# Spreading the DRAM sums of weight tiles over a two-layer decoder trunk, with one seven-product group moved from layer 0 to layer 1

## The chip, the cores and the metric

The kernel runs on one core of a Trainium2 chip. The metric is the device time of one execution in microseconds (us). Three runs of the kernel before took 819.1, 819.68 and 822.92 us; the median is 819.68.

## The reference

A residual stream x of 256 tokens by 1024 features goes through two layers, all in float32:

```python
for l in range(2):
    h = rms_norm(x, norm_mix[l])
    x = x + (short_conv_mixer(h) if l == 0 else moba_attention(h, shared K/V))
    x = x + mem_cross_attention(rms_norm(x, norm_mem[l]), rms_norm(mem, norm_memkv[l]))
    h = rms_norm(x, norm_ffn[l])
    g, u = split(h @ ffn_w_gu[l])          # 1024 x 5632: gate and up, 2816 each
    x = x + (silu(g) * u) @ ffn_w_down[l]  # 2816 x 1024
    if l == 0: shared K/V = rms_norm(x, kv_norm) @ w_kv, rotary on K
out = rms_norm(x, norm_final)
```

The change touches only the product h @ ffn_w_gu, the gate/up product of the two feed-forwards, and the transfers that prepare it.

## The kernel before

**Precision.** Every float32 operand is split into a high and a low part in fp32r; a product is three matmuls (low with high, high with low, high with high). A weight tile is loaded by SyncE as `raw` (512 KB), ScalarE casts it to `hi`, VectorE computes `lo` = raw - hi, and TensorE uses both. All matmuls have line 322, all work of ScalarE and VectorE has line 106 (helpers that record each operation), the weight loads line 339.

**Order of the work.** The program is written out by a planner at build time. `plan` is a list of 284 weight tiles ("items") in the order in which TensorE takes them, and `feed` loads, splits and hands them out. Up to five raw tiles and ten split pairs exist at a time (`RAWS`, `WBUFS`), so loads run ahead of TensorE by up to some ten to fifteen items. A clock model in the planner decides where in the streams of ScalarE and VectorE the splits stand; every engine then runs its stream strictly in order. `feed.hooks[n]` holds functions that are called right before the load of item n is issued; in this way other transfers are queued between loads. The items are: 0 to 63 the memory keys, convolution, memory values, query and output weights of layer 0; then the feed-forward of layer 0 (from 64 on); then 64 items for K, Q, V, memory keys (`memk1`), O, memory values, memory queries and output of layer 1; then the feed-forward of layer 1.

**The feed-forward.** The 2816 columns of gate and of up are cut into 11 pairs `jp` of 2 x 128 columns. Pairs 0 and 1 are computed by token rows (tiles `wr`), the others by columns (`wg` and `wu`, four items a pair). Between them stand the products with `ffn_w_down` (tiles `wd`, TensorE output `ff`), two pairs late; the last three pairs' down products follow at the end.

**Groups.** `GROUPS` names pairs that are computed two at a time, jp and jp + 1, with seven products instead of eight. The weights of a group make a 2 x 2 block matrix: `B11`, `B12` are gate and up columns for the upper 512 features, `B21`, `B22` those for the lower 512. A Strassen-like scheme (`seven`) takes three of the quarters as they are and four sums of them, T1 to T4, with sums S1 to S4 of the token activations on the other side. A group takes 14 weight tiles where two pairs take 8; the four down tiles of its two down products stand between them. Before, `GROUPS = (4, 8)` holds for both layers.

**The sums T1 to T4** don't depend on the input. They are built in DRAM by DMA, long before their group, in 16 steps of 512 KB for a group (`sum_steps`, 64 in all):

```python
order = (("T1", "B11", False), ("T3", "B12", False), ("T1", "B12", True), ("T3", "B22", True),
         ("T2", "T1", False), ("T2", "B22", True), ("T4", "T2", False), ("T4", "B21", True))
return [step(name, source, i, add) for name, source, add in order for i in range(2)]
```

A step with False is a plain DRAM-to-DRAM copy, issued by SyncE (line 453) in the same queue as the weight loads; one with True adds a quarter to a sum in DRAM, issued by GpSimd (line 452) with `accum_op`. An add waits for the copy that it adds to, and a copy of one sum from another waits for the adds of the first; the issuing engine stands while it waits. In the trace all sums are called `T`, and the tiles loaded from them `raw_wT`. GpSimd also computes the reciprocal roots of the norms (`rs`, line 106) and loads the stored activations of the memory for layer 1 (`mT`, line 1538, two halves).

Before, the steps hang at items 44 to 169: the first four copies of a group at four items in a row, then three items after each add, 32 items for a group.

Of the kernel before, what the change touches and what calls it, by code (L numbers as in the profile page):

```python
# [32 lines left out]
ROW_PAIRS = 2  # L33
# [6 lines left out]
HOLD = 300  # L40
AMPLE = 2
BANKWISE = 5
GROUPS = (4, 8)
SUMS_FROM = 44
SUM_GAP = 3


class Clock:
# [213 lines left out]
def yoco_kernel(  # L262
# [87 lines left out]
    def col_plan(name, w, c0):  # L350
        return [dict(name=f"{name}_{g}", src=w[g * 512:(g + 1) * 512, c0:c0 + T], a=4, b=T, gain=None, pieces=1,
                     halves=2) for g in range(2)]

    def pair_plan(name, w, c0):

        return [dict(name=f"{name}_{g}", a=2, b=2 * T, gain=None, pieces=1, halves=1,
                     src=[w[g * 256:(g + 1) * 256, c:c + T] for c in (c0, DFF + c0)]) for g in range(4)]
# [43 lines left out]
    def ffn_steps():  # L401

        steps = []
        for jp in range(NP):
            steps.append(("gu", jp))
            if ROW_PAIRS <= jp < NP - LAG + ROW_PAIRS:
                steps.append(("down", jp - ROW_PAIRS))
        return steps, list(range(NP - LAG, NP))
# [7 lines left out]
    def quarter(l, jp, name, i):  # L416
        kh, part = QUARTER[name]
        k = 4 * kh + 2 * i
        src = ffn_w_gu[l][k * P:(k + 2) * P, part * DFF + jp * T:part * DFF + jp * T + 2 * T]
        return src.rearrange("(a p) n -> p a n", p=P)  # L420

    def seven_plan(l, jp):
        plan = []
        for name in SEVEN:
            if name[:4] == "down":
                plan += down_plan(l, jp - ROW_PAIRS + int(name[4]))
                continue
            for i in range(2):
                it = dict(name=f"w{name}_{l}_{jp}_{i}", a=2, b=2 * T, gain=None, pieces=1, halves=1)
                if name[0] == "T":  # L430
                    it["sum"] = l, jp, name, i
                else:
                    kh, part = QUARTER[name]
                    k, c = 4 * kh + 2 * i, part * DFF + jp * T
                    it["src"] = ffn_w_gu[l][k * P:(k + 2) * P, c:c + 2 * T]
                plan.append(it)
        return plan
# [5 lines left out]
    def sum_steps(l, jp):  # L443
        for name in ("T1", "T2", "T3", "T4"):
            for i in range(2):
                weight_sums[l, jp, name, i] = aside.tile([P, 2, 2 * T], F32, name=f"{name}_{l}_{jp}_{i}")

        def step(name, source, i, add):
            dst = weight_sums[l, jp, name, i]
            src = weight_sums[l, jp, source, i] if source[0] == "T" else quarter(l, jp, source, i)  # L450
            if add:
                return lambda: nc.gpsimd.dma_start(dst, src, accum_op=OP.add)  # L452
            return lambda: nc.sync.dma_start(dst, src)
# [5 lines that stand above are left out]
    def down_plan(l, jp):  # L459
        return [dict(name=f"wd{l}_{k}", src=ffn_w_down[l][k * P:(k + 1) * P, :], a=1, b=D, gain=None, pieces=1,  # L460
                     halves=2) for k in (2 * jp, 2 * jp + 1)]

    def ffn_plan(l):
        steps, last = ffn_steps()
        plan = []
        for kind, jp in steps + [("down", jp) for jp in last]:
            if kind == "gu" and jp in GROUPS:
                plan += seven_plan(l, jp)
            elif kind == "gu" and jp - 1 in GROUPS or kind == "down" and \
                    any(jp + ROW_PAIRS - g in (0, 1) for g in GROUPS):  # L470
                pass
            elif kind == "gu" and jp < ROW_PAIRS:
                plan += pair_plan(f"wr{l}_{jp}", ffn_w_gu[l], jp * T)
            elif kind == "gu":
                plan += col_plan(f"wg{l}_{jp}", ffn_w_gu[l], jp * T)
                plan += col_plan(f"wu{l}_{jp}", ffn_w_gu[l], DFF + jp * T)
            else:
                plan += down_plan(l, jp)
        return plan
# [8 lines left out]
    plan += row_plan("cout", conv_w_out[0], 0) + row_plan("memv0", mem_w_kv[0], D, "memkv0")  # L488
    plan += q_plan(0) + row_plan("mo0", mem_w_o[0], 0)
    plan += ffn_plan(0)  # L490
    plan += row_plan("k1", w_kv, 0, "kv") + row_plan("q1", moba_w_q[0], 0, "mix1") + row_plan("v1", w_kv, D, "kv")
    plan += row_plan("memk1", mem_w_kv[1], 0, "memkv1", halves=2) + row_plan("o1", moba_w_o[0], 0)
    plan += row_plan("memv1", mem_w_kv[1], D, "memkv1")
    plan += q_plan(1) + row_plan("mo1", mem_w_o[1], 0)
    plan += ffn_plan(1)
    feed = side.feed = Feed(clock, plan, load_chunk, split_high, split_low)

# [452 lines left out]
    for k in range(KD):  # L950
        feed.hooks[36 + k] = [put_aside(k)]

    at = SUMS_FROM
    for l in range(2):
        for jp in GROUPS:
            for n, step in enumerate(sum_steps(l, jp)):
                feed.hooks.setdefault(at, []).append(step)
                at += SUM_GAP if n // 2 in (2, 3, 5, 7) else 1


    def short_conv(act, into):
# [175 lines left out]
    def swiglu(l, src, done, fine_end=False, at_end=None):  # L1137
# [8 lines left out]
        def gu_w(jp):  # L1146
            taken = {}

            def part(i):
                if i not in taken:  # L1150
                    taken[i] = [feed.take(f"{('wg', 'wu')[i]}{l}_{jp}_{g}") for g in range(2)]
                return taken[i]

            return part
# [41 lines left out]
        def gate_up(jp, w, jj):  # L1196
            u, j = unit_of(2 * jp + jj)
            pieces = [feat.tile([P, T], F32, tag=f"f{i}", name=f"gu_sb{i}") for i in range(2)]
            gus = []
            for i in range(2):  # L1200
                side.grab("gu")
                gus.append(gu_tile("gu"))
                mm_cols(gus[i], act, w(i), jj, 0)
            for i in range(2):
                mm_cols(gus[i], act, w(i), jj, 1)
                if jj:
                    feed.free(2)
                if i == 0:
                    gate = side.start(gate_steps(gus[0], pieces[0]))
                else:  # L1210
                    job = side.start(up_steps(gus[1], pieces, gate, u[:, j, 0, :], u[:, j, 1, :]))
            for h in range(2):
                guT.add_job(h, (2 * jp + jj) // 4, job)
# [170 lines left out]
        def down_w(jp):  # L1384
            return [feed.take(f"wd{l}_{2 * jp + i}") for i in range(2)]

        def down(jp, w, h, b, acc=None, c=(0, 512), first=0, end=NP - 1):
            for i in range(2):
                k = 2 * jp + i
                guT.need(k, (h,))  # L1390
                mm3(accs[h][b][:, c[0]:c[1]] if acc is None else acc, guT.parts(k, tok(h)),
                    [r[:, 0, b * 512 + c[0]:b * 512 + c[1]] for r in w[i]],
                    k == 2 * first, k == 2 * end + 1)
                side.poll()
# [6 lines left out]
        steps, last = ffn_steps()  # L1401
        sums_job = [side.start(token_sums())]
        for jp in range(ROW_PAIRS, NP):
            if jp in GROUPS:
                seven(jp)
            if jp in GROUPS or jp - 1 in GROUPS:
                continue
            w = gu_w(jp)
            n = jp - ROW_PAIRS
            gate_up(jp, w, 0)  # L1410
            wd = down_w(n) if ("down", n) in steps else None
            for h in range(2):
                if h == 1:
                    gate_up(jp, w, 1)
                for b in range(2 if wd else 0):
                    if h == b == 1:
                        feed.free(2)
                    down(n, wd, h, b)
# [186 lines left out]
    memv0 = mem_values("memv0", mT0)  # L1605
    mem_attention(0, memk0, memv0, in_mem0, in_ffn0)
    swiglu(0, in_ffn0, residual(in_moba))
    memk1, mT1 = moba(in_moba, in_mem1)
    memv1 = mem_values("memv1", mT1)
    mem_attention(1, memk1, memv1, in_mem1, in_ffn1)  # L1610
    swiglu(1, in_ffn1, finish, fine_end=True, at_end=lambda: fin.update(gain=load_gain(norm_final, "g_final")))


# [20 lines left out]
```

## Time and profile before

| | |
|---|---|
| median of three runs | 819.68 us |
| the profiled execution | 820.24 us |
| span of its trace | 818.5 us |
| TensorE busy, mean granted clock | 788.8 us (96%), 0.983 |
| VectorE, ScalarE, GpSimd busy | 580.4, 463.2, 51.8 us |
| DMA | 192.67 MB, 235 GB/s over the span |
| sums in DRAM | 16 + 16 copies by SyncE, 32 adds by GpSimd, 512 KB each |

In the rows of the trace PE is TensorE, DVE VectorE, ACT ScalarE, POOL GpSimd and SP SyncE; a q behind the name is the engine's sequencer, which issues DMAs. `out<-in` names what is written and what is read, without buffer numbers, and xN is the number of instructions. A row of the chain or of the timeline begins with its start and its length in us. In the timeline the brackets hold the time in which the engine stood before, and what ended it; "issue" there means that the profile shows nothing that it waited for. In a row of the stages stand the bounds, the length, then for PE, PEld (weight loads of TensorE), DVE, ACT and POOL the busy time and the number of instructions, then TensorE's granted clock (1.00 is full), the share of the 16 DMA engines that was busy, and GB/s.

### The profile page before, as it was taken

The page shows a single profiled execution, that of the slowest core. Times are in us where ns is not written, and L with a number is a line of the kernel's source. Part 1 is how long each engine was busy: PE and PEld are TensorE (multiplying, and loading weights), DVE is VectorE, ACT ScalarE, POOL GpSimd, SP SyncE. Part 2 cuts the span into 40 slices and gives each one's busy share as a digit, 9 for nine tenths or more (in the row PEclk, how much of TensorE's full clock was granted, in tenths as well). Part 3 has the DMA queues.
Part 4 walks back from the last instruction along what each step waited for, and adds up shares of the span by engine and source line. Part 5 has one row for each costly group of instructions (what it writes and reads, how often), then busy time and mean ns, then how long its engine had stood idle before and what let it go on. Part 6 is the DMA issues. An engine that isn't in the chain of part 4 may idle for free.

```text
span 818.5 us, 11285 instructions
## 1 busy us (share of the span) xinstructions
PE 788.8 (96%) x4141; PEld 672.5 (82%) x4141; DVE 580.4 (71%) x864; ACT 463.2 (57%) x721; POOL 51.8 (6%) x76
## 2 busy tenths in 40 slices
PE   9999999999989988996999999999999999999996
PEld 8988887898778867875788889988988788888885
DVE  5988786676676773676667566877767686966873
ACT  6765655665554643554556555655556555755751
POOL 0100011101110011011121100000000000000000
PEclk9999999999999988998999999999999999999999
DMA  9767799986988999899998942856543546965941
GB/s 333 224 213 230 245 319 226 370 216 155 284 227 277 306 321 297 215 358 289 342 281 252 253 172 97 263 204 203 205 134 104 185 151 216 323 206 189 330 150 51
DMA packets 99724, 192.67 MB, mean 235 GB/s; under 512 B 6669, under 2 KB 56917, under 8 KB 99157
## 3 DMA queue, kind: packets, MB, share of 16 engines
q1 hardware_dynamic: 90212, 172.54, 61.4%
q0 software_dynamic: 8992, 18.88, 12.9%
q8 instruction: 32, 0.52, 0.3%
q10 hardware_dynamic: 464, 0.53, 0.2%
q14 instruction: 24, 0.19, 0.1%
HBM read 188.78 MB, written 36.70 MB: 275 GB/s over the span
## 4 chain that ended last, share of the span: by engine, by line
PE 78%; DMA 12%; DVE 5%; ACT 2%; issue 2%; POOL 0%; SPq 0%; POOLq 0%; DVEq 0%; ACTq 0%
PE gu L322 15%; PE ff L322 11%; PE acc_memk L322 6%; PE q_acc L322 5%; PE cu L322 5%; PE acc_mo L322 5%; PE seven L322 5%; DMA raw_wd<-in_ffn_w_down_dram 4%; PE acc_memv L322 4%; PE pb L322 3%; PE acc_k L322 3%; PE acc_o L322 3%; DMA raw_wu<-in_ffn_w_gu_dram 3%; PE po L322 2%; DMA raw_wg<-in_ffn_w_gu_dram 2%; PE acc_v L322 2%
## 5 line engine op out<-in xcount | busy, mean ns | idle before, releaser
L322 PE MATMUL ff<-hi_wd,guT 128*128 128x512 f32 (+1 forms) x352 | 109.0, 391 | 0.0
L322 PEld LDWEIGHTS ff<-hi_wd,guT 128*128 128x128 f32 x352 | 66.9, 191 | 13.4
L322 PE MATMUL ff<-lo_wd,guT 128*128 128x512 f32 (+1 forms) x176 | 69.4, 394 | 0.0
L106 ACT CAST hi_wd<-raw_wd 128x1024 fp32r<-128x1024 f32 x44 | 46.1, 1050 | 19.4 <-DMA raw_wd<-in_ffn_w_down_dram 17.9
L106 DVE TENSOR_TENSOR lo_wd<-raw_wd,hi_wd 128x1024 fp32r<-128x1024 f32 x44 | 53.4, 1218 | 5.0 <-ACT hi_wd L106 4.5
L452 POOL DMA_DIRECT2D T<-in_ffn_w_gu_dram x32 | 33.9, 1059 | 268.8 <-issue 137.0
L106 DVE TENSOR_TENSOR gu_sb<-gu_sb,gu 128x256 f32<-128x256 f32 x40 | 16.6, 419 | 46.7 <-ACT gu_sb L106 46.5
L322 PE MATMUL gu<-ffn,hi_wg 128*128 128x512 f32 x160 | 44.2, 415 | 4.6 <-DVE gu_sb L106 4.6
L322 PE MATMUL acc_memk<-mT,hi_memk 128*128 128x256 f32 x256 | 47.0, 289 | 0.0
L106 ACT COPY gu_sb<-gu 128x256 f32<-128x256 f32 x40 | 14.7, 372 | 53.6 <-PE gu L322 53.4
L106 DVE TENSOR_TENSOR lo_wT<-raw_wT,hi_wT 128x1024 fp32r<-128x1024 f32 x32 | 38.2, 1220 | 8.2 <-ACT hi_wT L106 8.2
L322 PE MATMUL gu<-ffn,hi_wu 128*128 128x512 f32 x160 | 41.9, 406 | 0.0
L106 POOL TENSOR_TENSOR rs<-ms,neg_half 128x1 f32<-128x1 f32 x14 | 13.3, 948 | 448.6 <-DVE ms L106 447.1
L322 PE MATMUL acc_mo<-hi_mo,oT_mem 128*128 128x512 f32 x128 | 41.2, 397 | 0.2 <-DVE oT_mem L106 0.2
L322 PEld LDWEIGHTS gu<-ffn,hi_wg 128*128 128x128 f32 x160 | 31.2, 199 | 11.6 <-DVE gu_sb L106 5.4
L106 ACT CAST hi_wT<-raw_wT 128x1024 fp32r<-128x1024 f32 x32 | 33.1, 1052 | 12.6 <-DMA raw_wT<-T 12.4
L322 PEld LDWEIGHTS acc_memk<-mT,hi_memk 128*128 128x128 f32 x256 | 40.0, 196 | 0.2
L322 PE MATMUL gu<-hi_wr,ffn 128*128 128x512 f32 x128 | 39.8, 392 | 0.0
L322 PE MATMUL acc_memv<-hi_memv,mT 128*128 128x512 f32 x128 | 39.7, 391 | 0.0
L106 DVE TENSOR_TENSOR lo_wu<-raw_wu,hi_wu 128x1024 fp32r<-128x1024 f32 x28 | 33.7, 1220 | 8.0 <-ACT hi_wu L106 8.0
L322 PEld LDWEIGHTS ff<-lo_wd,guT 128*128 128x128 f32 x176 | 33.7, 191 | 6.6
L106 ACT CAST hi_wu<-raw_wu 128x1024 fp32r<-128x1024 f32 x28 | 29.3, 1051 | 15.4 <-DMA raw_wu<-in_ffn_w_gu_dram 13.0
(271 smaller groups left out, 2033.3 us busy)
## 6 DMA issues: line engine op xcount, KB each, us to landing
raw_wd<-in_ffn_w_down_dram SPq DMA_DIRECT2D x44, 512.0 KB, 6.0
T<-in_ffn_w_gu_dram POOLq DMA_DIRECT2D x32, 512.0 KB, 8.9
raw_wT<-T SPq DMA_DIRECT2D x32, 512.0 KB, 5.7
raw_wB<-in_ffn_w_gu_dram SPq DMA_DIRECT2D x24, 512.0 KB, 4.8
raw_wg<-in_ffn_w_gu_dram SPq DMA_DIRECT2D x20, 512.0 KB, 5.0
raw_wu<-in_ffn_w_gu_dram SPq DMA_DIRECT2D x20, 512.0 KB, 5.9
raw_memv<-in_mem_w_kv_dram SPq DMA_DIRECT2D x16, 512.0 KB, 5.3
T<-in_ffn_w_gu_dram SPq DMA_DIRECT2D x16, 512.0 KB, 8.8
```

What stands on the lines that cost most here:

```text
L106: return call(out, *args, **kw)
L322: nc.tensor.matmul(o, l, r, start=start, stop=stop)
L452: return lambda: nc.gpsimd.dma_start(dst, src, accum_op=OP.add)
```

## The change

Three things change. `GROUPS` becomes one tuple for each layer: layer 0 has the group at pair 8 only, its pairs 4 and 5 are computed as plain pairs; layer 1 has groups at pairs 4, 6 and 8, so that three groups follow one another there. There are four groups as before, and the 284 items remain 284; the feed-forward of layer 0 has 72 items instead of 78, that of layer 1 84 instead of 78. The 64 steps keep their order within a group, and the groups their order by layer and pair, but step n now hangs at item 44 + int(3.2 n): the last at item 245, in the feed-forward of layer 1, instead of 169. Everything else follows from that.

```diff
-GROUPS = (4, 8)
+GROUPS = ((8,), (4, 6, 8))
 SUMS_FROM = 44
-SUM_GAP = 3
+SUM_GAP = 3.2
...
-            if kind == "gu" and jp in GROUPS:
+            if kind == "gu" and jp in GROUPS[l]:
                 plan += seven_plan(l, jp)
-            elif kind == "gu" and jp - 1 in GROUPS or kind == "down" and \
-                    any(jp + ROW_PAIRS - g in (0, 1) for g in GROUPS):
+            elif kind == "gu" and jp - 1 in GROUPS[l] or kind == "down" and \
+                    any(jp + ROW_PAIRS - g in (0, 1) for g in GROUPS[l]):
                 pass
...
-    at = SUMS_FROM
-    for l in range(2):
-        for jp in GROUPS:
-            for n, step in enumerate(sum_steps(l, jp)):
-                feed.hooks.setdefault(at, []).append(step)
-                at += SUM_GAP if n // 2 in (2, 3, 5, 7) else 1
+    steps = [step for l in range(2) for jp in GROUPS[l] for step in sum_steps(l, jp)]
+    for n, step in enumerate(steps):
+        feed.hooks.setdefault(SUMS_FROM + int(SUM_GAP * n), []).append(step)
...
-            if jp in GROUPS:
+            if jp in GROUPS[l]:
                 seven(jp)
-            if jp in GROUPS or jp - 1 in GROUPS:
+            if jp in GROUPS[l] or jp - 1 in GROUPS[l]:
                 continue
```

## The prediction

> **What bounds the kernel now.** I read the page's totals first, then the busy time of each engine by stage, then the chain of waits in order of time, then DMA queue by queue in the two feed-forward stages.
>
> ```profile
> span 818.5 us, 11285 instructions
> PE 788.8 (96%) x4141; PEld 672.5 (82%) x4141; DVE 580.4 (71%) x864; ACT 463.2 (57%) x721; POOL 51.8 (6%) x76
> ```
>
> TensorE is busy for 96% of the span, which says little, since a wait can hide in a modelled end. The next view cuts the span into stages: first the feed-forward of layer 0, from its second gate/up bank on, then two stages up to the feed-forward of layer 1, and the same stretch of that. After the times come the number of instructions, and at the end TensorE's granted clock, the share of the 16 DMA engines' time, and GB/s.
>
> ```profile
> 215.76:419.93 204.17, 185.20 (x856) 152.83 (x855) 132.18 (x165) 104.84 (x149) 21.60 (x21) 0.94 0.95 289
> 419.93:526.90 106.97, 106.57 (x621) 92.73 (x621) 70.16 (x134) 60.77 (x101) 6.85 (x7) 1.00 0.71 223
> 526.90:638.93 112.03, 111.86 (x591) 95.16 (x591) 83.47 (x127) 65.79 (x108) 4.87 (x4) 1.00 0.53 173
> 638.93:812.05 173.12, 173.10 (x860) 145.88 (x859) 126.85 (x166) 96.70 (x141) 0.55 (x1) 1.00 0.60 203
> ```
>
> The bounds of the two long rows are read from the chain of waits; both feed-forwards have groups 4 and 8 and the same products, and start and end alike:
>
> ```profile
> 215.76 5.94 PE gu L322 x26
> 416.94 2.99 PE ff L322 x13
> 638.93 5.94 PE gu L322 x26
> 809.88 2.17 PE ff_end L322 x18
> ```
>
> The same work takes 204.17 us in layer 0 and 173.12 us in layer 1: 31.05 us more. Of these, 204.17 - 185.20 = 18.97 us is a standing TensorE, and a mean clock of 0.94 over 204.17 us is another 12.3 us; together 31.2. In the second long row nothing is lost, and 0.4 and 0.2 us in the two between. So what can be won lies in layer 0's feed-forward. The chain shows what it waits for:
>
> ```profile
> 225.70 8.52 DMA raw_wu<-in_ffn_w_gu_dram
> 286.74 8.90 DMA raw_wg<-in_ffn_w_gu_dram
> 302.48 12.12 DMA raw_wu<-in_ffn_w_gu_dram
> 317.31 8.72 PE gu L322 x32
> 328.78 5.54 PE gu L322 x32
> 372.85 10.13 DMA raw_wd<-in_ffn_w_down_dram
> 385.84 8.60 DMA raw_wd<-in_ffn_w_down_dram
> ```
>
> Weight loads. The 8.72 us beside 5.54 us for the same 32 matmuls is the price of a stall after its end: 3.2 us at a lower clock. The Trainium skill (TensorE: Matmul & The Clock Gate, Part 1) says that the clock halves after an idle window of about 3.4 us and comes back after as much busy time; the trace agrees in kind, and by that rule stalls that stay under 3.4 us would carry no such surcharge.
>
> DMA in the two stages: queues (packets, MB, share of the 16 engines), then issues with their median time to landing; layer 0 first.
>
> ```profile
> q1 hardware_dynamic: 21625, 48.92, 65.9%
> q0 software_dynamic: 5168, 9.96, 28.6%
> T<-in_ffn_w_gu_dram POOLq DMA_DIRECT2D x20, 512.0 KB, 8.9
> raw_wd<-in_ffn_w_down_dram SPq DMA_DIRECT2D x20, 512.0 KB, 8.7
> ```
>
> ```profile
> q1 hardware_dynamic: 17596, 34.91, 59.7%
> raw_wd<-in_ffn_w_down_dram SPq DMA_DIRECT2D x20, 512.0 KB, 4.7
> ```
>
> Prices per transfer of 512 KB (0.524 MB): an add from GpSimd takes 0.286 x 204.17 = 58.4 us for 9.96 MB, or 19 adds: 3.07 us of all 16 engines. A load or a plain DRAM copy takes 0.659 x 204.17 / 93.3 = 1.44 us in layer 0 and 0.597 x 173.12 / 66.6 = 1.55 us in layer 1; I take 1.5. Layer 0's demand, 193 us at 0.95, does not fit into the 173 us that TensorE needs; layer 1's, 103 us, does.
>
> **The change part by part.** *One group fewer in layer 0, one more in layer 1.* A group against two plain pairs: from the chain the down half of a pair in layer 1 (the gate/up half of 5.54 us is shown above), and the stage row of layer 1's group 4:
>
> ```profile
> 669.04 2.75 PE ff L322 x12
> 688.36:720.30 31.94, 31.94 (x145) 26.14 (x144) 29.23 (x32) 21.89 (x25) 0.00 (x0) 1.00 0.88 298
> ```
>
> A pair is 2 x (5.54 + 2.75) = 16.58 us, two are 33.16, a group is 31.94. So layer 0 gets 1.2 us more TensorE work, layer 1 1.2 less: zero in sum. Six loads (14 weight tiles for 8) move from layer 0 to layer 1.
>
> *The steps are spread.* Before, a group's 16 steps hung at 32 consecutive loads, the first four copies at four loads in a row. The SyncE queue in layer 0's feed-forward, loads of pair 7 (wg, wu), with copies for group 4 of layer 1:
>
> ```order
> L339 DMA raw_wd0_9_3122<-in_ffn_w_down_dram 128x1024
> L453 DMA T1_1_4_0_578<-in_ffn_w_gu_dram 256x1x512
> L339 DMA raw_wg0_7_0_3127<-in_ffn_w_gu_dram 128x4x256
> L453 DMA T1_1_4_1_579<-in_ffn_w_gu_dram 256x1x512
> L339 DMA raw_wg0_7_1_3157<-in_ffn_w_gu_dram 128x4x256
> L453 DMA T3_1_4_0_582<-in_ffn_w_gu_dram 256x1x512
> L339 DMA raw_wu0_7_0_3168<-in_ffn_w_gu_dram 128x4x256
> L453 DMA T3_1_4_1_583<-in_ffn_w_gu_dram 256x1x512
> L339 DMA raw_wu0_7_1_3186<-in_ffn_w_gu_dram 128x4x256
> ```
>
> The same copies in the changed kernel, one pair earlier in the same stage:
>
> ```order
> L453 DMA T1_1_4_0_570<-in_ffn_w_gu_dram 256x1x512
> L339 DMA raw_wd0_7_2926<-in_ffn_w_down_dram 128x1024
> L339 DMA raw_wg0_6_0_2937<-in_ffn_w_gu_dram 128x4x256
> L339 DMA raw_wg0_6_1_2949<-in_ffn_w_gu_dram 128x4x256
> L453 DMA T1_1_4_1_571<-in_ffn_w_gu_dram 256x1x512
> L339 DMA raw_wu0_6_0_2982<-in_ffn_w_gu_dram 128x4x256
> L339 DMA raw_wu0_6_1_3047<-in_ffn_w_gu_dram 128x4x256
> L339 DMA raw_wd0_8_3064<-in_ffn_w_down_dram 128x1024
> L453 DMA T3_1_4_0_574<-in_ffn_w_gu_dram 256x1x512
> ```
>
> Three loads pass between two copies instead of one. The longest DMA wait of the stage, 12.12 us from 302.48 on, falls on such a four, whose last copy SyncE issued right behind that load:
>
> ```profile
> 303.09 2.10 SPq L453 DMA_DIRECT2D T<-in_ffn_w_gu_dram  x1
> ```
>
>
> *Demand of layer 0's feed-forward.* Loads run some 10 items ahead of TensorE. Before, the stage issued items 78 to 151: 74 loads, 17 copies, 19 or 20 adds. Now it ends earlier in the list, at about item 145: 68 loads, and steps 11 to 31 of the 64 (positions 44 + 3.2n), 10 copies and 11 adds. (68 + 10) x 1.5 + 11 x 3.07 = 151 us, against 173.1 + 1.2 = 174.3 us of TensorE: 0.87 of the engines. It fits, so the 31.05 us go, as far as no part of the stage is overloaded by itself.
>
> *The densest part of layer 0* is its group 8: 18 loads, 3 copies, 2 adds in 31.9 us, (18 + 3) x 1.5 + 2 x 3.07 = 37.6, or 5.7 us too much. What covers this is the lead of the loads over their use. SyncE's rows in layer 1 (the last two of the four wT are T4's), the T1 and T4 products on the chain, and the page's two splits of such a tile:
>
> ```profile
> 675.65 1.47 SPq L339 DMA_DIRECT2D raw_wT<-T  x2
> 694.60 5.82 SPq L339 DMA_DIRECT2D raw_wT<-T  x4
> 696.53 2.80 PE seven L322 x12
> 713.74 2.72 PE seven L322 x12
> L106 ACT CAST hi_wT<-raw_wT 128x1024 fp32r<-128x1024 f32 x32 | 33.1, 1052 | 12.6 <-DMA raw_wT<-T 12.4
> L106 DVE TENSOR_TENSOR lo_wT<-raw_wT,hi_wT 128x1024 fp32r<-128x1024 f32 x32 | 38.2, 1220 | 8.2 <-ACT hi_wT L106 8.2
> ```
>
> T1's lead is 21 us, T4's, issued by 700.4, 13 us. A load lands in 4.7 us when the engines are free and 8.7 when they are not, and its two splits take 1.05 and 1.22 us: slack 2 to 6 us at the end of a group. I leave 3 us of stall here, bounds 0 and 5.7 plus 3.2 for the clock, 8.9.
>
> *Layer 1's feed-forward* now issues 70 loads, 4 copies and 6 adds: 74 x 1.5 + 6 x 3.07 = 129 us of 171.9: it fits too. Its densest part is group 4: 18 loads, copies at 236 and 239, adds at 232, 242 and 245: 20 x 1.5 + 9.2 = 39.2 in 31.9 us, 7.3 too much; group 6 behind it has no steps left and needs 27.0. I leave 3 us, bounds 0 and 7.3 + 3.2 = 10.5. VectorE carries the splits of three groups in a row; in the row of group 4 above it is busy for 29.23 of 31.94 us and TensorE never stands, so a third group in the row is carried, but a late load can be made up by 2.7 us per group only.
>
> *The stages between* get 19 or 20 steps in 64 loads, (64 + 10) x 1.5 + 10 x 3.07 = 142 us in 219: 1 us for single late loads, bounds 0 and 4.
>
> *Layer 0's start.* One stall of 1.5 us stands in front of the feed-forward, where VectorE waits for a small load that is queued behind the bunched copies:
>
> ```profile
> 122.91 9.13 DMA pos_i<-in_positions_dram
> PE acc_memv L322 <- DVE lo_memv L106: 1.5, 1, 1.5
> ```
>
> With one copy fewer ahead, and loads between them, I take 1 us off, bounds 0 and 1.5.
>
> *GpSimd's queue.* Each add there must wait for its copy, and adds in a row follow one another slowly:
>
> ```profile
> 216.47 1.07 POOL L452 DMA_DIRECT2D T<-in_ffn_w_gu_dram  x1 [4.94 <-DMA T<-in_ffn_w_gu_dram]
> 225.63 1.06 POOL L452 DMA_DIRECT2D T<-in_ffn_w_gu_dram  x1 [8.08 <-issue]
> 489.47 0.56 POOL L1538 DMA_DIRECT2D mT<-mem_aside  x1 [26.10 <-ACT hi_memk L106]
> ```
>
> Two adds start 9.16 us apart. What is queued behind a waiting add are the rs of the norms and the two loads of the memory activations. In the changed GpSimd queue, between the norm after layer 0 and that before layer 1's memory attention:
>
> ```order
> L106 TENSOR_TENSOR rs_4117<-ms_4120,neg_half_100 128x1
> L452 DMA T1_1_6_0_578<-in_ffn_w_gu_dram 256x1x512
> L452 DMA T1_1_6_1_579<-in_ffn_w_gu_dram 256x1x512
> L1535 DMA mT1_0_4477<-mem_aside_0_560 128x2048
> L452 DMA T3_1_6_0_582<-in_ffn_w_gu_dram 256x1x512
> L1535 DMA mT1_1_4773<-mem_aside_1_561 128x2048
> L452 DMA T3_1_6_1_583<-in_ffn_w_gu_dram 256x1x512
> L452 DMA T2_1_6_0_580<-in_ffn_w_gu_dram 256x1x512
> ```
>
> Before, both mT loads stood behind all adds; now one add stands between them. mT's second half already waited 26.10 us for something else, so one add of 9.16 us is covered. I cost it at 0.
>
> *Sum.* The profiled execution took 820.24 us (span 818.5 and 1.7 around it), 0.56 above the median of 819.68. 820.2 - 31.05 - 1 + 3 + 3 + 1 = 795.
>
> **The rivals.** *Layer 1 pays back.* Group 4 there, under the last sums, stalls as a group of layer 0 does now. Two of the 20 us slices of layer 0:
>
> ```profile
> 220.00:240.00 20.00, 17.25 (x85) 14.01 (x84) 13.56 (x19) 10.53 (x15) 2.11 (x2) 1.00 1.05 288
> 380.00:400.00 20.00, 12.76 (x54) 10.33 (x54) 13.38 (x16) 10.87 (x14) 1.82 (x2) 0.83 1.06 342
> ```
>
> Without the 2.75 us that TensorE stands in the first slice, before any group, layer 0 loses 28 us to two groups, 14 each. One such: 788 + 14 + 4 = 806. For it speaks the 39.2 us in 31.9; against it that the fours of copies are gone. *GpSimd's queue makes mT late:* two adds instead of none ahead of the second half, 9.2 us: 804. *Slower than before:* each of the three groups in a row costs 14 us, and so does the one left in layer 0: 788 + 56 = 844. It decides if a load costs over 31.9 / 18 = 1.77 us of the engines throughout layer 1's groups, or VectorE cannot keep up over 96 us; the 1.55 us and the 29.23 of 31.94 speak against both. *No change:* layer 0's feed-forward is not held by the sums at all; 820. The Trainium skill (DMA: Bandwidth & Descriptors, Measured) gives some 425 GB/s for a core that streams alone; by it 59 MB would take an estimated 139 us and the stage would not be bound by bytes. The slice with 1.06 of the engines' time at 342 GB/s while TensorE stands speaks against it: bytes are not what is short, engine time is.
>
> **How the numbers follow.** The forecast, 787 to 800: 0.62. Layer 1 pays back, 800 to 814: 0.23. GpSimd's queue, 797 to 806: 0.07. No change: 0.04. Slower: 0.04. A measurement of this kernel can tell about 0.5%, 4.1 us, from no change. Faster by more: 0.62 + 0.23 + 0.07 = 0.92; same 0.04; slower 0.04. The low end is every stall gone, 820.2 - 31.05 - 1.5 = 787.7; the high end takes in half of the second case: 807.
>
> **What would show it.** Right: layer 0's stage falls to about 178 us, its clock to 1.00 and its DMA share to under 0.9; layer 1's stays between 171 and 175 with a share near 0.75; loads of wd land in 5 to 7 us in both. Wrong: a clock under 0.97 in either stage, DMA waits over 6 us on the chain between layer 1's groups 4 and 6, or acc_memk waiting for mT.

## The result and the profile after

The changed kernel takes 807.81 us (median of four runs, 807.05 to 809.99), the kernel before 820.08 beside it: a ratio of 0.985 with a 95% interval of 0.982 to 0.988. So it is 12 us faster, clear of noise, but only half of the 25 us that were forecast, and 0.8 us outside the range. The profiled execution took 807.05 us; first its page, then the stages of the prediction, found again by their first and last pieces of the chain:

```profile
span 805.3 us, 11271 instructions
PE 782.5 (97%) x4141; PEld 667.9 (83%) x4141; DVE 579.6 (72%) x864; ACT 462.1 (57%) x721; POOL 51.6 (6%) x76
```

```profile
215.68:400.57 184.89, 178.80 (x891) 150.96 (x891) 123.50 (x164) 98.87 (x152) 12.05 (x12) 0.98 0.83 255
400.57:622.31 221.74, 218.51 (x1212) 187.89 (x1211) 153.81 (x260) 127.03 (x208) 18.03 (x17) 1.00 0.70 224
622.31:798.87 176.56, 173.46 (x824) 143.73 (x823) 134.51 (x167) 101.58 (x138) 6.86 (x7) 0.99 0.78 249
```

Layer 0's feed-forward falls from 204.17 to 184.89 us (-19.3), the two stages between rise from 219.0 to 221.74 (+2.7), layer 1's feed-forward from 173.12 to 176.56 (+3.4). 820.24 - 19.3 + 2.7 + 3.4 is 807.0: the three rows account for the whole result. In layer 0's stage the DMA engines are now busy for 0.83 of the time, and yet it is some 10 us longer than the 174.3 us of TensorE work that the prediction counted. The chain of waits in the order of time shows where: in group 8 of layer 0 (the first three rows), behind the memory keys of layer 1 (the fourth), and in group 4 of layer 1 (the last).

```profile
335.93 7.66 DMA raw_wd<-in_ffn_w_down_dram
346.03 7.90 DMA raw_wT<-T
368.63 6.45 DMA raw_wd<-in_ffn_w_down_dram
502.08 10.61 DMA raw_memv<-in_mem_w_kv_dram
688.53 9.73 DMA raw_wd<-in_ffn_w_down_dram
```

SyncE's queue around the first two of them has a long stretch with two loads only, and then copies of sums between the loads:

```profile
323.68 8.93 SPq L339 DMA_DIRECT2D raw_wB<-in_ffn_w_gu_dram  x2
335.19 0.51 SPq L453 DMA_DIRECT2D T<-T  x1
341.48 0.50 SPq L453 DMA_DIRECT2D T<-T  x1
```

The engines' use in slices of 10 us (last but one column), with the group's first product at 331.91 us:

```profile
325.00:335.00 10.00, 10.00 (x53) 8.61 (x52) 5.24 (x8) 6.18 (x10) 0.00 (x0) 1.00 0.32 102
335.00:345.00 10.00, 10.00 (x46) 8.14 (x45) 6.56 (x7) 5.18 (x7) 1.04 (x1) 1.00 0.97 348
345.00:355.00 10.00, 9.23 (x40) 7.11 (x38) 6.32 (x6) 6.06 (x7) 1.05 (x1) 1.00 1.06 344
355.00:365.00 10.00, 6.58 (x22) 5.38 (x23) 8.92 (x11) 5.78 (x8) 0.00 (x0) 0.66 1.11 352
```

Just ahead of the group the engines are used for a third of the time. SyncE waits there for a raw tile, but not for a late landing: the four tiles loaded from 317 us on landed after 5.4 and 5.7 us (medians), and ScalarE began to split them only at 328.72 us, after 5.53 us of waiting for TensorE. Then the engines are full for 30 us, and in that stretch TensorE stands, from 354.2 us on.

TensorE does not wait there for a weight tile of its own. It waits to transpose `u`, a sum of products that VectorE computes and that TensorE needs in the middle of the T3 product. In VectorE's stream `u` stands behind the two splits of the T4 tiles, which wait for their loads. First the changed kernel, then layer 1's group 4 before the change, with the same order and no stall:

```profile
355.08 1.23 DVE L106 TENSOR_TENSOR lo_wT<-raw_wT,hi_wT 128x1024 fp32r<-128x1024 f32 x1 [0.75 <-ACT hi_wT L106]
357.67 0.69 DVE L106 TENSOR_TENSOR u<-u,g 128x512 f32<-128x512 f32 x1
358.42 1.11 PE L326 MATMUL pt_g<-ident,u 128*128 128x128 f32 x4 [4.19 <-DVE u L106]
```

```profile
705.13 2.36 DVE L106 TENSOR_TENSOR lo_wT<-raw_wT,hi_wT 128x1024 fp32r<-128x1024 f32 x2 [0.41 <-ACT hi_wT L106]
709.22 0.69 DVE L106 TENSOR_TENSOR u<-u,g 128x512 f32<-128x512 f32 x1
710.37 0.60 PE L326 MATMUL pt_g<-ident,u 128*128 128x128 f32 x4
```

### The profile page after: what moved, and what is told of

Its sections match the earlier page's. It is cut to its first block, busy times and chain, and to the rows that moved or that the text cites. A ratio compares the mean times of both kernels' runs of the same rounds, so it can differ in the third digit from the quotient of the medians.

```text
span 805.3 us, 11271 instructions
## 1 busy us (share of the span) xinstructions
PE 782.5 (97%) x4141; PEld 667.9 (83%) x4141; DVE 579.6 (72%) x864; ACT 462.1 (57%) x721; POOL 51.6 (6%) x76
## 4 chain that ended last, share of the span: by engine, by line
PE 77%; DMA 11%; DVE 6%; ACT 3%; issue 2%; POOL 0%; POOLq 0%; ACTq 0%; DVEq 0%; SPq 0%
PE gu L322 15%; PE ff L322 12%; PE seven L322 6%; PE cu L322 6%; PE acc_mo L322 5%; PE q_acc L322 5%; PE acc_memk L322 4%; DMA raw_wd<-in_ffn_w_down_dram 3%; PE pb L322 3%; PE acc_v L322 3%; PE acc_q L322 3%; PE acc_k L322 3%; PE acc_memv L322 3%; DMA raw_wT<-T 2%; PE s L322 2%; PE po L322 2%
## 5 line engine op out<-in xcount | busy, mean ns | idle before, releaser
L322 PE MATMUL gu<-ffn,hi_wg 128*128 128x512 f32 x160 | 40.8, 393 | 1.5 <-DVE gu_sb L106 1.4
L322 PE MATMUL gu<-ffn,hi_wu 128*128 128x512 f32 x160 | 39.6, 390 | 0.0
L106 ACT CAST hi_wu<-raw_wu 128x1024 fp32r<-128x1024 f32 x28 | 29.5, 1052 | 11.9 <-DMA raw_wu<-in_ffn_w_gu_dram 6.5
```

The costliest lines, as they stand in the source:

```text
L106: return call(out, *args, **kw)
L322: nc.tensor.matmul(o, l, r, start=start, stop=stop)
```

## The experiments

**Two theories.** *Engine time*, as in the prediction: a group stalls when loads and steps need more time of the 16 DMA engines than the group lasts, less what the lead of the loads covers. *The ring of raw tiles:* a raw tile is free for the next load only when it has landed and both splits (1.05 and 1.22 us) are done, so five raw tiles deliver at best one tile in (landing + 2.3) / 5 us. A group takes 18 tiles in 31.94 us, 1.77 us each; beyond a landing of 5 x 1.77 - 2.3 = 6.6 us it stalls, whatever share of the engines is free. Each kernel is timed beside the kernel before.

**e1: the sums left out.**

```diff
-            load(raw, weight_sums[it["sum"]])
+            l, jp, name, i = it["sum"]
+            load(raw, quarter(l, jp, dict(T1="B11", T2="B22", T3="B12", T4="B21")[name], i))
...
-    steps = [step for l in range(2) for jp in GROUPS[l] for step in sum_steps(l, jp)]
-    for n, step in enumerate(steps):
-        feed.hooks.setdefault(SUMS_FROM + int(SUM_GAP * n), []).append(step)
```

> The changed kernel without the 64 sum steps; the tiles T1 to T4 are loaded from plain quarters of the weights instead, so the output is not the reference's. Loads, splits and matmuls stay. If the sums in flight cause every stall that is left (both the ring theory, five raw tiles with loads that land too late, and the engine-time theory, too much DMA in a group), the time is 788 to 791: layer 0's feed-forward stage 174 to 176 us, layer 1's 172 to 174. If three groups in a row overload VectorE by themselves, layer 1's stage stays at 176.6 us and the time is 792 to 795.

789.66 us. So the sums in flight cost the changed kernel 18 us. Layer 0's stage and layer 1's:

```profile
214.12:391.06 176.94, 176.39 (x892) 149.43 (x891) 123.37 (x164) 98.45 (x152) 0.55 (x1) 1.00 0.61 202
609.35:782.64 173.29, 172.16 (x825) 142.52 (x823) 134.41 (x167) 101.36 (x138) 0.55 (x1) 1.00 0.66 221
```

Three groups in a row do not overload VectorE: in the second row TensorE stands for 1.1 us.

**e2: seven raw tiles.** One split pair (a `hi` and a `lo`) makes room for two raw tiles.

```diff
-RAWS = 5
-WBUFS = 10
+RAWS = 7
+WBUFS = 9
```

> The changed kernel with 7 raw tiles instead of 5 and 9 split pairs instead of 10 (16 tiles of lead instead of 15). Ring theory: a group takes a tile each 1.77 us, so 5 raw tiles bear a landing time of 5 x 1.77 - 2.3 = 6.6 us and 7 bear 10.1 us; the stalls in layer 0's group 8 and layer 1's group 4 shrink to under 2 us each, 795 to 799 us. Engine-time theory: the excess demand of 5.7 and 7.3 us in these groups is as before and one tile more of lead is worth 1.8 us each at most: 804 to 808 us.

794.10 us, with all sums where the change puts them: 1 us under the ring theory's range, 10 under that of engine time. The issues in and around layer 0's group 8 show that this is not because a load takes less time; first the changed kernel (318 to 376 us), then e2 (314 to 370 us), the last column the median time to landing:

```profile
raw_wT<-T SPq DMA_DIRECT2D x8, 512.0 KB, 6.2
raw_wd<-in_ffn_w_down_dram SPq DMA_DIRECT2D x8, 512.0 KB, 6.9
raw_wg<-in_ffn_w_gu_dram SPq DMA_DIRECT2D x2, 512.0 KB, 7.2
```

```profile
raw_wT<-T SPq DMA_DIRECT2D x8, 512.0 KB, 6.0
raw_wd<-in_ffn_w_down_dram SPq DMA_DIRECT2D x8, 512.0 KB, 8.4
raw_wg<-in_ffn_w_gu_dram SPq DMA_DIRECT2D x2, 512.0 KB, 10.8
```

With seven tiles more loads are under way at once, those of `wd` and `wg` take longer (8.4 us against 6.9, 10.8 against 7.2), those of `wT` do not, and the stage is shorter all the same (first row; the second is the two stages between):

```profile
214.21:393.70 179.49, 176.99 (x891) 149.28 (x891) 123.15 (x164) 98.47 (x152) 11.06 (x11) 1.00 0.84 263
393.70:612.00 218.30, 218.10 (x1211) 187.92 (x1211) 153.68 (x260) 126.30 (x208) 17.16 (x17) 1.00 0.71 225
```

179.49 us with a share of 0.84, where the changed kernel has 184.89 and 0.83. Two things changed at once, though: e2 has 16 tiles in all instead of 15, and its splits stand elsewhere in the streams. e8 and e12 take this apart.

**e3: the groups alone.** The steps hang as before, groups as in the change.

```diff
+    at = SUMS_FROM
+    for l in range(2):
+        for jp in GROUPS[l]:
+            for n, step in enumerate(sum_steps(l, jp)):
+                feed.hooks.setdefault(at, []).append(step)
+                at += 3 if n // 2 in (2, 3, 5, 7) else 1
```

> Only the groups are moved (8 in layer 0; 4, 6, 8 in layer 1); the steps hang as in the kernel before, 32 items a group with the first four copies at four items in a row, items 44 to 169. Engine-time theory: layer 0's stage has 6 loads fewer, 9 us of 193, still 10 us more than TensorE needs: 809 to 814 us. Ring theory: one group instead of two meets late loads in layer 0, so half of the 28 us goes: 804 to 810 us, and layer 1's stage, free of sums, is at 172 to 174 us.

811.26 us, a ratio of 0.990 (0.986 to 0.994). Layer 0's stage and layer 1's:

```profile
216.09:407.95 191.86, 179.39 (x892) 151.52 (x891) 123.33 (x164) 98.97 (x152) 19.39 (x19) 0.97 0.95 288
628.39:801.64 173.25, 171.49 (x824) 142.71 (x823) 134.59 (x167) 101.58 (x138) 0.55 (x1) 1.00 0.66 221
```

The time is in the range of engine time, but only 1.3 us above that of the ring. The share in layer 0 stays at 0.95, which speaks for engine time as the limit there.

**e4: the spacing alone.** Groups 4 and 8 in both layers, a step at every second item.

```diff
-GROUPS = ((8,), (4, 6, 8))
-SUM_GAP = 3.2
+GROUPS = ((4, 8), (4, 8))
+SUM_GAP = 2
```

> Only the spacing: groups 4 and 8 in both layers as before, one step at every second item from 44 to 170, so as dense as before but without fours of copies in a row. Engine-time theory: the demand of layer 0's stage is the same 193 us, 817 to 821 us. If the fours of copies make the long landing times: 806 to 812 us.

814.50 us, 0.990 (0.987 to 0.993), between the two forecasts. Layer 0's stage:

```profile
214.11:413.54 199.43, 181.63 (x856) 150.57 (x855) 132.43 (x165) 104.42 (x149) 20.43 (x20) 0.96 0.95 295
```

4.7 us are gained there without a byte less, so the spacing is worth that much; the rest of the stage's excess stays, at the same share.

**e5: seven raw tiles in the kernel before** (the same edit as e2).

> The kernel before with 7 raw tiles and 9 split pairs. Its layer 0 stage needs 193 us of the DMA engines for 173 us of TensorE. If engine time is what binds there, the stage cannot get under 190 us and the time is 804 to 816 us; if the ring of raw tiles binds there too (median landing 8.7 us, 7 tiles bear 10.1), the stage falls to 176 to 184 us and the time to 792 to 800 us.

816.98 us, 0.998 (0.995 to 1.001), no change that can be told and 1 us above what engine time allowed. Its layer 0 stage:

```profile
221.56:420.00 198.44, 182.49 (x860) 150.92 (x859) 132.01 (x166) 104.61 (x150) 20.53 (x20) 0.96 0.96 297
```

At a share of 0.96 more raw tiles bring 5.7 of 204 us in that stage, and it begins 5.8 us later. So before the change engine time binds, and more raw tiles cannot help.

**e6: steps outside the groups, five raw tiles.**

```diff
+    free = [*range(44, 112), *range(134, 168), *range(186, 224)]
     for n, step in enumerate(steps):
-        feed.hooks.setdefault(SUMS_FROM + int(SUM_GAP * n), []).append(step)
+        feed.hooks.setdefault(free[n * len(free) // len(steps)], []).append(step)
```

> The changed kernel with the 64 steps spread evenly over items 44 to 111, 134 to 167 and 186 to 223, so none is issued while loads of a group, or of the weights after the memory keys, are in flight; 5 raw tiles. Ring theory: loads in the groups land in 4 to 6 us, no stall is left there, 790 to 795 us. If it is the sum of the bytes in a stage and not the moment that counts, layer 0's pairs, now with a step at every 2.2 items, lose what the groups gain: 802 to 808 us.

799.03 us: 9 us better than the change, 4 more than forecast. In layer 0's group 8 the loads now land in time (314 to 370 us):

```profile
raw_wd<-in_ffn_w_down_dram SPq DMA_DIRECT2D x9, 512.0 KB, 4.3
raw_wT<-T SPq DMA_DIRECT2D x8, 512.0 KB, 4.7
```

and no stall is left in any group. This does not tell the theories apart, since the groups also have less to transfer. The 4 us lie in the places where steps stand closer now, above all in the two stages between:

```profile
393.48:617.35 223.87, 220.76 (x1212) 189.07 (x1211) 154.01 (x260) 127.01 (x208) 20.26 (x19) 0.99 0.73 222
```

**e7: both**, the edits of e2 and e6.

> Both: steps outside the groups and 7 raw tiles with 9 split pairs. With the stalls gone already by either one, no more than what is left above the kernel without sums (789.7) can be won: 788 to 793 us.

791.88 us, 0.967 (0.963 to 0.972): with e2 the best of the versions that compute the reference, 2 us above the kernel without sums. Its two feed-forwards:

```profile
216.31:392.98 176.67, 176.50 (x891) 149.36 (x891) 123.17 (x164) 98.40 (x152) 11.07 (x11) 1.00 0.86 270
611.32:783.08 171.76, 171.58 (x824) 142.67 (x823) 135.04 (x168) 101.54 (x139) 2.65 (x3) 1.00 0.69 235
```

**e8 and e12: is it the raw tiles, or the number of tiles ahead?** e8 has 5 raw tiles and 9 pairs, 14 in all; e12 has 7 and 8, 15 in all as the change.

```diff
-WBUFS = 10
+WBUFS = 9     # e8
...
-RAWS = 5
-WBUFS = 10
+RAWS = 7      # e12
+WBUFS = 8     # e12
```

> Control for the 7 raw tiles: 5 raw tiles as in the changed kernel and 9 split pairs instead of 10. If the gain came from the raw tiles, this is no faster than the changed kernel: 807 to 815 us. If it came from the planner's other order with 9 pairs, 794 to 800 us.

804.55 us: a little under the range. The three stages show more than the total:

```profile
215.65:397.31 181.66, 177.80 (x891) 150.46 (x891) 123.65 (x164) 98.54 (x152) 12.05 (x12) 0.99 0.84 260
397.31:615.65 218.34, 218.15 (x1212) 187.89 (x1211) 154.00 (x260) 126.73 (x208) 17.15 (x17) 1.00 0.71 227
615.65:794.48 178.83, 173.77 (x825) 143.71 (x823) 135.76 (x168) 102.78 (x139) 6.86 (x7) 0.99 0.76 249
```

With five raw tiles layer 0's stage is 3.2 us shorter than in the changed kernel (e2: 5.4), the two stages between 3.4 (as in e2), and layer 1's 2.3 longer.

> The changed kernel with 7 raw tiles and 8 split pairs: 15 tiles in all, as in the changed kernel. If it is the raw tiles (how many loads can be under way at once) that let the groups keep their pace, 794 to 800 us. If it is the number of tiles ahead of TensorE that counts, this is where the changed kernel is, 805 to 810 us.

796.08 us, 12 us less than the changed kernel with the same 15 tiles in all. Layer 0's stage and layer 1's:

```profile
214.26:396.13 181.87, 178.65 (x891) 150.33 (x891) 123.46 (x164) 98.51 (x152) 12.12 (x12) 0.99 0.83 260
615.14:788.11 172.97, 171.94 (x825) 142.61 (x823) 136.56 (x169) 102.95 (x140) 6.86 (x7) 1.00 0.77 255
```

In layer 1 the raw tiles are what counts: 172.97 us with seven, 178.83 and 176.56 with five. In layer 0 they are not: seven raw tiles leave the stage as long as e8's five. Here are e12's slices at the same places of the group as those of the changed kernel above (its first product is at 330.74 us):

```profile
323.80:333.80 10.00, 10.00 (x53) 8.60 (x52) 5.21 (x8) 6.15 (x10) 0.00 (x0) 1.00 0.32 109
333.80:343.80 10.00, 10.00 (x46) 8.15 (x44) 8.76 (x9) 7.91 (x10) 1.04 (x1) 1.00 0.97 349
343.80:353.80 10.00, 9.26 (x40) 7.14 (x38) 6.37 (x7) 4.53 (x6) 0.93 (x1) 1.00 1.06 344
353.80:363.80 10.00, 8.03 (x30) 6.55 (x31) 8.56 (x11) 5.90 (x7) 0.13 (x1) 0.83 1.10 350
```

The pause ahead of the group is the same, and behind it the engines move the same bytes in the same time: the loads are issued earlier and land no earlier, `wg` after 11.8 us in the median instead of 7.2. The first `wg` tile is split 24.1 us after the group's first product, 23.6 in the changed kernel and 25.0 in e8. In e2, with 16 tiles, it is 21.0: one tile more of lead. What e8 and e12 share is the planner's order: `u` stands behind one of the two T4 splits, not both. The wait for it in e12:

```profile
355.77 0.66 PE L326 MATMUL pt_g<-ident,u 128*128 128x128 f32 x4 [2.71 <-DVE u L106]
```

In e8 it is 3.83 us, against 4.19, and another of 1.45 us that the changed kernel has at 375.5 is gone in both. No run changes this order alone, so its share of the 3 us is not shown.

**e9 and e10: four raw tiles**, with the sums and without.

```diff
-RAWS = 5
+RAWS = 4
```

> The changed kernel with 4 raw tiles instead of 5. Ring theory: a group then bears a landing of 4 x 1.77 - 2.3 = 4.8 us, and its loads land in 6 to 7 us beside the sums: (6.5 + 2.3) / 4 = 2.2 us a tile, 18 x 0.43 = 8 us more in each group under the sums, and stalls at other late loads: 816 to 830 us. Engine-time theory: one tile less of lead, 1.8 us each: 809 to 812 us.

825.45 us, 1.007 (1.004 to 1.010) of the kernel before: 17.6 us more than five raw tiles, and a little slower than before the change. e8, which has 14 tiles in all too, takes 804.55.

> The changed kernel without the sum steps (tiles T loaded from plain quarters, so not the reference's output) and with 4 raw tiles. Loads in the groups land in 4.1 to 5.6 us without the sums, at the 4.8 us that 4 raw tiles bear: ring theory 790 to 798 us, so the fourth tile costs far less here than with the sums. If 4 raw tiles are slow by themselves (the planner's order), the cost is as large as with the sums.

797.38 us, 7.7 more than e1, at the upper end of what was expected. One raw tile less costs under half as much where loads land early. Layer 1's stage:

```profile
612.06:789.61 177.55, 173.27 (x825) 142.03 (x823) 134.93 (x167) 101.77 (x138) 0.55 (x1) 1.00 0.67 219
```

It is 4.3 us longer than e1's at nearly the same share, 0.67 and 0.66, so here the ring slows a stage whose engines have time to spare.

**e11: adds as copies.**

```diff
             if add:
-                return lambda: nc.gpsimd.dma_start(dst, src, accum_op=OP.add)
+                return lambda: nc.sync.dma_start(dst, src)
```

> The changed kernel with every add replaced by a plain copy by SyncE at the same place, so the sums are wrong quarters and the output is not the reference's; 64 copies, no adds, GpSimd's queue free. If the adds (3.07 us of the engines each instead of 1.5) lengthen the loads' landing: 796 to 802 us. If any step does so by being queued between the loads: 804 to 810 us.

796.81 us. Of the 18 us that the sums still cost, 11 go with the adds; 7 stay with twice as many plain copies.

## Why the prediction was wrong, point by point

**What bound the kernel: right.** Layer 0's feed-forward lost its 31 us to engine time under the sums: in e5 its share stays at 0.96 and 5.7 us are gained, and e1, without sums, stands for 0.6 us.

**The prices and the demand: right**, layer 1's demand within 7%. In the changed kernel's layer 0 stage the queues are

```profile
q1 hardware_dynamic: 21071, 40.96, 63.6%
q0 software_dynamic: 3160, 6.08, 19.2%
```

0.636 x 184.89 us for 40.96 MB is 1.50 us a load or copy, 0.192 x 184.89 for 6.08 MB is 3.06 us an add; the demand is 0.83 x 184.89 = 153 us (151 forecast). Layer 1's is 0.78 x 176.56 = 138 us (129 forecast).

**The group moved: a small miss.** Forecast at 1.2 us more in layer 0 and 1.2 less in layer 1. In e7, which has hardly a stall in either stage, layer 0 needs 176.67 and layer 1 171.76 us: 3.6 more and 1.4 less than 173.12. Why one group saves 3.6 us and a third only 1.4 was not tried.

**The step that failed: "I leave 3 us of stall here"**, the slack of 2 to 6 us that the lead was to give layer 0's group 8. There the stage is 184.89 - 176.67 = 8.2 us above e7's, near the 8.9 of the upper bound, in which the lead covers nothing. With the 2.4 us of the point before, this is 7.6 of the 12 us by which the forecast missed. The excess of engine time was right: the engines are full for 30 us in the group, and e12 moves no byte sooner with two more raw tiles. The slack was wrong. It was counted up to TensorE's T4 product, in layer 1 at 713.74 us. But TensorE needs `u` before that, at 710.37, and `u` stands in VectorE's stream behind the T4 splits. There the last T4 tile waited 0.43 us for its split, VectorE stood for 0.27 us behind the splits, and `u` was ready 0.46 us before its use: some 1.2 us to spare, not 2 to 6. In the changed kernel the last T4 load is issued 14.1 us after the group's first product (346.03 - 331.91) where in layer 1 before it was 11.7, and takes 7.9 us instead of 4.5: 5.8 us late. Less 1.2 that leaves 4.6, and TensorE stands for 4.19. Of the 8.2 us, 5.9 are a standing TensorE (4.19, then 1.45 at 375.5 us, and small ones), and 2.3 are matmuls at a lower clock. That the sums cause the lateness is shown (e1, e7); that another order in VectorE's stream would hide it was not tried.

**Layer 1's group 4, the same term:** 3 us forecast, 176.56 - 171.76 = 4.8 measured. Here the ring has a part that the prediction left out: a late landing also keeps its raw tile, and so delays the load five places on; seven raw tiles (e12) take 3.6 of the 4.8 us away. The rest was not followed up. The rival "layer 1 pays back" had the time in its range (800 to 814), but not for its reason: layer 1 paid 3.4 us, the larger part stayed in layer 0.

**The stages between:** 1 us forecast, 2.7 measured; the 10.61 us load at 502.08 in the chain above, behind copies of group 6's sums. In e2 and e8 the excess is gone (218.3 us), in e8 with five raw tiles, so the ring is not its cause; what is stays open.

**Layer 0's start:** 1 us less forecast, nothing measured. The small load lands sooner, but TensorE stands for 1.23 us later on, for `q`, and the chain leads there through another load:

```profile
123.08 6.82 DMA pos_i<-in_positions_dram
143.17 9.81 DMA raw_mo<-in_mem_w_o_dram
```

**GpSimd's queue: right, at no cost.** The second half of mT still waits for ScalarE, not for the add ahead of it:

```profile
469.43 0.57 POOL L1535 DMA_DIRECT2D mT<-mem_aside  x1 [40.90 <-ACT hi_memk L106]
```

**Three groups in a row on VectorE: right**, e1 and e3. The rival "slower than before" did not come up, nor did "no change".

**The signs.** The shares under 0.9 and the landings of `wd` (medians of 6.4 and 5.6 us) came as they should if right; the stage lengths and layer 0's clock of 0.98 did not, and one sign of being wrong came up, the 9.73 us wait on the chain in layer 1's group 4.

**Short stalls were not free.** The prediction let stalls under 3.4 us carry no lower clock. Its own slow piece, the 8.72 us at 317.31, follows a stand of 2.96 us:

```profile
317.31 3.78 PE L322 MATMUL gu<-ffn,hi_wg 128*128 128x512 f32 x8 [2.96 <-DVE gu_sb L106]
```

The sum by its terms: layer 0 missed by 7.6 us, layer 1 by 1.7 (176.56 against 174.9), the stages between by 1.7, the start by 0.9; together 11.9, from 795 to 807.

## What to carry to other kernels

First find what the stalled engine itself waits for. The chain named a weight load, but TensorE stood for `u`, which another engine's fixed order had put behind that load's split; a slack counted to the tile's own use was too long by that.

A stage whose DMA engines have time to spare can still wait for DMA: with n landing buffers it gets at best one tile in (landing + what is done before the buffer is free) / n (e10, and layer 1 in e12). More buffers need not help: in layer 0's group 8 the engines were full, the landings grew with the loads under way, and the tiles came no sooner (e12).

Spreading background transfers helps as far as engine time binds; then keep them out of the dense stretches (e6) or give more landing buffers and lead, here at the cost of one pair of finished tiles (e2). The two together took 791.88 us where the change took 807.81.

## What was not expected of the hardware

An accumulating DMA in DRAM takes 3.06 us of all 16 engines for 512 KB, twice a load's 1.50 (the prediction had 3.07), and most of the cost that remains goes with these adds (e11: 796.81 us without). A load of 512 KB that lands in 4.3 us in a group without sums beside it takes 6.9 us with them, and 8.4 with two more loads under way; e2 is the faster kernel all the same.
